# Ordering each engine's queue of a hybrid decoder block with a build-time list scheduler instead of hand-merged program order

## The chip, the cores and the metric

The kernel runs on the 8 cores of one Trainium2 chip. Each core works on two of the 16 sequences and the cores do not talk to each other. The metric is the device time of the slowest core, in microseconds (us). Executions of these kernels fall into two states: in the slow one the cores of a die show a lower granted TensorE clock and the time is longer (in the changed kernel 0.85 against 0.96, and 1918 against 1739 us). A median quoted is over all executions, slow ones included.

Names used below: PE is TensorE, DVE is VectorE, ACT is ScalarE, POOL is GpSimd, SP is SyncE, which here only issues DMAs. The traces here show each of them taking its queue in the order in which the program filled it. An operation at the head that waits for a semaphore holds up what stands behind it, ready or not: the example below is a wait of 41.55 us for one small constant.

## The reference

One layer, d_model 1024, 16 sequences of 2048 tokens behind 16 shared meta tokens:

```python
h = concat(meta_tokens, x)
u = rms_norm(h, norm_mix_g) @ w_in                     # 2576 columns
c_val, c_gate, q, k, v, g, gate_lr = split(u)
y_conv = conv_group(c_val, c_gate, ...)                # GLU, depthwise conv of 31, LayerNorm, swish
y_gla  = gla_group(q, k, v, g, gate_lr, ...)           # gated linear attention, 4 heads, state carried along
h = h + concat(y_conv, y_gla) @ w_out
h = h + (silu(n @ w_gate) * (n @ w_up)) @ w_down       # n = rms_norm(h, norm_ffn_g), hidden 2816
y = rms_norm(h, norm_final_g)
```

"Mixer" below is everything up to `w_out`, "feed-forward" the rest.

## The kernel before

A core handles 8 blocks of 512 tokens. Every operation is recorded with the buffers that it reads (R) and writes (W); the recorder derives its dependencies and appends it to its engine's queue at once, so a queue has the order of the Python program:

```python
    def add(self, eng, fn, R=(), W=(), dkey=None):
        op = Op(eng, fn, dkey is not None, dkey)
        ...                                    # deps: last writers and readers of R and W
        if eng == "pool" and fn is not None and dkey is None:
            if self.last_pool is not None:
                deps[id(self.last_pool)] = self.last_pool
            self.last_pool = op
        ...
        self.ops[eng].append(op)
```

The mixer of block b+1 does not depend on the feed-forward of block b, so the two are woven together by hand: lists of units with costs, merged so that the mixer's units fall between 15% and 93% of the feed-forward's cost.

```python
def merge(main, side, f0, f1):
    ...
    for c, fn in main:
        while i < len(side) and mt and done / mt >= f0 + (f1 - f0) * sdone / st_:
            out.append(side[i][1])
            ...
        out.append(fn)
        done += c
...
            plan = [fn for _, fn in mixer(0, blocks[0][0], True, True, False)]
            for b in range(nb):
                f = ffn(b % 2, blocks[b][0])
                m = mixer((b + 1) % 2, ...) if b + 1 < nb else []
                plan += merge(f, m, 0.15, 0.93) if m else [fn for _, fn in f]
            for fn in plan:
                fn()
```

A feed-forward unit, and the state chain of the mixer:

```python
P.add("pe", mm8(pg[:], ...), R=[Bwg] + Bx2T, W=[Bpg])            # 8 matmuls 128x512
P.add("pe", mm8(pu[:], ...), R=[Bwu] + Bx2T, W=[Bpu])
P.add("act", ... out=th, in_=pg, func=AF.Tanh)
P.add("dve", ... out=th, in0=th, in1=pg)                         # ftmp in the profile
P.add("dve", ... out=actT[:, j, :], in0=th, in1=pu)              # actT
# state chain, for each of four 128-token tiles
P.add("pool", ... out=Rbd[rows, t, :, hh, :], in0=S, in1=em2)    # twice
P.add("dve", ... out=U[:, hp, :], in0=S, in1=pkv)                # twice
P.add("dve", ... out=S[:, hp, :], in0=U)                         # twice
```

The program uses PSUM (the memory that matmuls write to) as eight tiles of 128x512 f32, called banks here: four for the feed-forward, four in rotation for the mixer. The feed-forward and the mixer each have a ring of four weight tiles in SBUF. The weights are read as f32 once, written back to HBM as bf16, and read as bf16 from then on. At the end of a block its four tiles of `h` are normalized and stored; then the `h` of the block after next is loaded into the same buffers.

Of the kernel before, what the change touches and what calls it, by code (L numbers as in the profile page):

```python
# [6 lines left out]
F32 = mybir.dt.float32  # L7
BF16 = mybir.dt.bfloat16
I32 = mybir.dt.int32
AF = mybir.ActivationFunctionType  # L10
# [14 lines left out]
LN_EPS = 1e-5  # L25
NWM, NWF = 4, 4
NW = NWM + NWF
RSQRT_MAGIC = 1597463007.0

W_GATE, W_VAL, W_Q, W_K, W_V, W_G, W_O, W_FG, W_FU, W_FD = 0, 2, 4, 5, 6, 8, 10, 14, 25, 36  # L30
# [3 lines left out]
class Buf:  # L34
    def __init__(self, name, psum=False):
        self.name = name
        self.lw = None
        self.rd = []
        self.psum = psum


class Op:
    __slots__ = ("eng", "fn", "deps", "sig", "ticket", "dma", "dkey", "dval")

    def __init__(self, eng, fn, dma, dkey):
        self.eng = eng
# [6 lines left out]
        self.dval = 0  # L53


class Prog:
    ENGS = ("pe", "act", "dve", "pool", "sp")

    def __init__(self):
        self.ops = {e: [] for e in self.ENGS}  # L60
        self.dcount = {}
        self.last_pool = None

    def add(self, eng, fn, R=(), W=(), dkey=None):
        op = Op(eng, fn, dkey is not None, dkey)
        deps = {}
        for b in R:
            if b.lw is not None:
                deps[id(b.lw)] = b.lw
            if b.psum:  # L70
                for r in b.rd:
                    if r.eng != eng:
                        deps[id(r)] = r
        for b in W:
            if b.lw is not None:
                deps[id(b.lw)] = b.lw
            for r in b.rd:
                deps[id(r)] = r
        if eng == "pool" and fn is not None and dkey is None:
            if self.last_pool is not None:  # L80
                deps[id(self.last_pool)] = self.last_pool
            self.last_pool = op
        deps.pop(id(op), None)
        op.deps = list(deps.values())
        for b in R:
            b.rd.append(op)
        for b in W:
            b.lw = op
            b.rd = []
        if op.dma:  # L90
            self.dcount[dkey] = self.dcount.get(dkey, 0) + 16
            op.dval = self.dcount[dkey]
        self.ops[eng].append(op)
        return op

    @staticmethod
    def _needs_wait(a, b):
# [43 lines left out]
def merge(main, side, f0, f1):  # L141

    mt = sum(c for c, _ in main)
    st_ = sum(c for c, _ in side)
    out, done, i = [], 0.0, 0
    sdone = 0.0
# [3 lines that stand above are left out]
            sdone += side[i][0]  # L150
            i += 1
        out.append(fn)
        done += c
    out.extend(fn for _, fn in side[i:])
    return out


def build_program(nseq, seqlen):
# [3 lines left out]
    nc = bass.Bass("TRN2", target_bir_lowering=False)  # L162
# [16 lines left out]
    out = nc.dram_tensor("out", [ntok, D], F32, kind="ExternalOutput").ap()  # L179
# [3 lines left out]
    with es:  # L183
        def sb(name, shape, dt=F32):
            return es.enter_context(nc.sbuf_tensor(name, list(shape), dt))
# [30 lines left out]
        sto = sb("sto", [128, 2, 6, 8])  # L216
        wring = [sb(f"wring{i}", [128, 2048], BF16) for i in range(NW)]
        gmix = sb("gmix", [128, D])
# [33 lines left out]
        def build(wseq):  # L252

            P = Prog()
# [33 lines left out]
            Bmt = [Buf(f"mt{i}") for i in range(4)]  # L288
            Bw = [Buf(f"w{i}") for i in range(NW)]
            Bwsc = [Buf(f"wsc{i}") for i in range(N_WT)]  # L290
# [110 lines left out]
            for s_ in range(4):  # L401
                P.add("dve", lambda e, s_=s_: e.tensor_copy(out=id4[s_ * 32:(s_ + 1) * 32, :],
                                                            in_=identf[s_ * 32:(s_ + 1) * 32, s_ * 32:(s_ + 1) * 32]),
# [24 lines left out]
            def newton_col(stt, Bst_, scale, eps):  # L428
# [3 lines left out]
                P.add("dve", lambda e: e.tensor_scalar(out=y.bitcast(I32), in0=a.bitcast(I32), scalar1=-0.5,  # L432
                                                       scalar2=RSQRT_MAGIC, op0=ALU.mult, op1=ALU.add), R=[Bst_], W=[Bst_])
                P.add("dve", lambda e: e.tensor_scalar(out=b, in0=a, scalar1=-0.5, scalar2=None, op0=ALU.mult),
# [8 lines left out]
            def newton_row(v, B_, scale, eps):  # L443
# [4 lines left out]
                P.add("dve", lambda e: e.tensor_scalar(out=y.bitcast(I32), in0=a.bitcast(I32), scalar1=-0.5,  # L448
                                                       scalar2=RSQRT_MAGIC, op0=ALU.mult, op1=ALU.add), R=[B_], W=[B_])
                P.add("dve", lambda e: e.tensor_scalar(out=b, in0=a, scalar1=-0.5, scalar2=None, op0=ALU.mult),  # L450
# [591 lines left out]
            plan = [fn for _, fn in mixer(0, blocks[0][0], True, True, False)]  # L1042
            for b in range(nb):
                f = ffn(b % 2, blocks[b][0])
                m = mixer((b + 1) % 2, blocks[b + 1][0], blocks[b + 1][1], False, True) if b + 1 < nb else []
                plan += merge(f, m, 0.15, 0.93) if m else [fn for _, fn in f]
            for fn in plan:
                fn()
            P.add("pool", None, W=Bh[0] + Bh[1] + Bwsc)
            return P, order  # L1050

        _, wseq = build(None)
        P, _ = build(wseq)
        P.finalize()
        esem = {e: es.enter_context(nc.semaphore(f"sem_{e}")) for e in Prog.ENGS}
        dsem = {k: es.enter_context(nc.semaphore(f"dsem_{k}")) for k in sorted(P.dcount)}
# [82 lines left out]
```

## Time and profile before

| before | us |
|---|---|
| median of the first 3 runs (the slowest is a slow one) | 2212.15 (2206.46 to 2273.65) |
| start to the first output store | 526.7 |
| block, store to store (middle of the run) | 254 to 256 |
| first store of the last block to the end | 17.6 |

From the page: the busy times, the busy share of PE in 40 slices with its granted clock, and the chain of waits that ended last. (Of 8498 matmuls 8340 have a record here.)

```profile
PE 1640.5 (74%) x8340; PEld 740.6 (34%) x8498; DVE 888.3 (40%) x1950; ACT 512.7 (23%) x808; POOL 201.7 (9%) x262
...
PE   0374768886897769877797768968697877977894
...
PEclk9885769998899889988898989989898988988997
...
PE 51%; DVE 19%; issue 13%; ACT 6%; DMA 5%; SPq 2%; POOL 2%; DVEq 1%; ACTq 0%; POOLq 0%
```

PE is the busiest engine and yet stands still a quarter of the time, in every slice a little, and its granted clock is below 0.9 in 22 of the 40 slices.

How PE loses time in a block, from its timeline:

```profile
1180.85 0.64 PE L836 MATMUL ps<-v_tm,k_tm 128*64 128x128 bf16 x16 [0.83 <-DVE k_tm L796]
1181.65 3.40 PE L486 MATMUL ps<-x2T,wring 128*128 128x512 bf16 x15 [0.16 <-issue]
1184.98 0.40 PE L808 MATMUL ps<-q_in,k_in 64*128 64x128 bf16 x8
1188.81 3.57 PE L486 MATMUL ps<-wring,xT 128*128 128x512 bf16 x8 [3.43 <-DVE U L851]
1198.59 1.86 PE L1011 MATMUL ps<-wring,actT 128*128 128x512 bf16 x4 [6.20 <-DVE actT L995]
```

The gate projection at 1188.81 waits 3.43 us for a bank that DVE's U operations free. After it, eight matmuls take 3.57 us at a granted clock of 0.50 (elsewhere eight take 1.89 us at 1.00), and then PE waits 6.20 us until DVE has made the last actT. DVE's timeline of the same stretch shows why actT is late:

```profile
1186.10 0.80 DVE L851 SCALAR_TENSOR_TENSOR U<-S,emid,ps 128x128 f32<-128x128 f32 x2
1187.08 0.68 DVE L855 TENSOR_SCALAR S<-U,csb 128x128 f32<-128x128 f32 x2 [0.18 <-DVE U L851]
...
1192.58 0.80 DVE L851 SCALAR_TENSOR_TENSOR U<-S,emid,ps 128x128 f32<-128x128 f32 x2
1194.15 2.79 DVE L855 TENSOR_SCALAR S<-U,csb 128x128 f32<-128x128 f32 x2 [0.77 <-POOL Rbd L845]
1196.86 0.67 DVE L993 SCALAR_TENSOR_TENSOR ftmp<-ftmp,ps 128x512 f32<-128x512 f32 x1
1197.64 0.69 DVE L995 SCALAR_TENSOR_TENSOR actT<-ftmp,ps 128x512 bf16<-128x512 f32 x1
```

The feed-forward's two operations, 1.4 us of work that PE needs, stand behind the whole state chain of the mixer, which itself pauses for POOL.

The start has its own loss. SP's queue, then the DVE operation that waited for it (start, length, what, and in brackets the idle time before it and what ended it):

```profile
22.55 30.82 SPq L326 DMA_DIRECT2D wsc<-wring  x8
...
55.66 0.43 SPq L353 DMA_DIRECT2D gng<-gla_norm_g  x1
```

```profile
58.27 0.17 DVE L410 TENSOR_SCALAR gb<-gb 128x2 f32<-128x2 f32 x1 [41.55 <-DMA gng<-gla_norm_g]
```

Eight write-backs, each waiting for its weight tile, stand ahead of five small constants. DVE waits 41.55 us for the last one, and the norms, and so PE (first matmul at 62.72 us), wait behind that DVE operation.

### The profile page before, as it was taken

The numbers are of one execution on the slowest core, as the hardware profiler recorded it, in microseconds if no ns is written. First come the engines' busy times: TensorE is split into PE (matmuls) and PEld (weight loads), VectorE is DVE, ScalarE is ACT, GpSimd is POOL, SyncE is SP. The second block draws the span as 40 slices with busy tenths as digits, with TensorE's granted clock in tenths as the row PEclk, the third lists the DMA queues.
The fourth block names the chain that finished last, engine by engine and source line by source line (L and its number), as shares of the span: only waits on it lengthen the run. The fifth ranks groups of instructions, "written<-read, shape, count | busy, mean of one in ns | idle before, by whom it ended". The sixth has DMA issues, their size and how long they took to land.

```text
span 2205.6 us, 27514 instructions; the slowest of 8 cores (2185.8 to 2205.6 us)
## 1 busy us (share of the span) xinstructions
PE 1640.5 (74%) x8340; PEld 740.6 (34%) x8498; DVE 888.3 (40%) x1950; ACT 512.7 (23%) x808; POOL 201.7 (9%) x262
## 2 busy tenths in 40 slices
PE   0374768886897769877797768968697877977894
PEld 0231323332333324333343333433243333433341
DVE  1225332544336342454325443363425443254422
ACT  0131222212231132312231122312222122312210
POOL 1012000300011000210002000110002000110000
PEclk9885769998899889988898989989898988988997
DMA  9242358775432245224342344323452343422442
GB/s 229 63 107 67 81 152 193 188 179 184 133 113 100 96 153 175 96 82 147 118 163 83 121 160 145 114 78 115 143 183 77 105 161 113 140 79 84 151 154 86
DMA packets 93488, 281.93 MB, mean 128 GB/s; under 512 B 12576, under 2 KB 29344, under 8 KB 93344
## 3 DMA queue, kind: packets, MB, share of 16 engines
q1 hardware_dynamic: 76928, 220.84, 30.6%
q0 software_dynamic: 16416, 59.32, 11.6%
q8 instruction: 72, 1.18, 0.2%
q14 instruction: 72, 0.59, 0.1%
HBM read 245.70 MB, written 41.94 MB: 130 GB/s over the span
## 4 chain that ended last, share of the span: by engine, by line
PE 51%; DVE 19%; issue 13%; ACT 6%; DMA 5%; SPq 2%; POOL 2%; DVEq 1%; ACTq 0%; POOLq 0%
PE ps L486 35%; PE ps L1011 10%; DMA wring<-wpack 4%; PE ps L631 2%; SPq L584 2%; DVE y_tm L905 2%; ACT xn_tm L462 1%; POOL Rbd L845 1%; PE ps L649 1%; DVE stn L437 1%; DVE xn_tm L465 1%; DVEq L131 1%; DVE S L855 1%; DVE csb L678 1%; PE ps L477 1%
## 5 line engine op out<-in xcount | busy, mean ns | idle before, releaser
L486 PE MATMUL ps<-x2T,wring 128*128 128x512 bf16 x2739 | 664.4, 399 | 93.2 <-DVE ftmp L993 69.3
L486 PEld LDWEIGHTS ps<-x2T,wring 128*128 128x128 bf16 x2816 | 282.6, 102 | 462.9 <-issue 182.9
L1011 PE MATMUL ps<-wring,actT 128*128 128x512 bf16 x1370 | 342.0, 405 | 55.1 <-DVE actT L995 43.3
L993 DVE SCALAR_TENSOR_TENSOR ftmp<-ftmp,ps 128x512 f32<-128x512 f32 x176 | 120.8, 686 | 401.6 <-ACT ftmp L992 401.6
L1011 PEld LDWEIGHTS ps<-wring,actT 128*128 128x128 bf16 x1408 | 142.9, 103 | 240.1 <-issue 103.3
L477 PE MATMUL ps<-ident,xn_tm 128*128 128x128 bf16 x520 | 50.0, 253 | 223.8 <-DVE stn L430 133.4
L992 ACT ACTIVATE ftmp<-ps 128x512 f32<-128x512 f32 x176 | 104.0, 595 | 426.2 <-PE ps L486 419.6
L486 PE MATMUL ps<-xT,wring 128*128 128x512 bf16 x751 | 194.0, 413 | 11.1 <-ACT xT L480 9.2
L486 PE MATMUL ps<-wring,xT 128*128 128x512 bf16 x497 | 134.5, 417 | 30.0 <-DVE U L851 29.1
L995 DVE SCALAR_TENSOR_TENSOR actT<-ftmp,ps 128x512 bf16<-128x512 f32 x176 | 121.1, 688 | 67.3 <-PE ps L486 63.3
L486 PE MATMUL ps<-wring,yT 128*128 128x512 bf16 x503 | 130.6, 411 | 0.7 <-issue 0.2
L477 PEld LDWEIGHTS ps<-ident,xn_tm 128*128 128x128 bf16 x520 | 39.5, 113 | 238.9 <-issue 234.1
L486 PEld LDWEIGHTS ps<-xT,wring 128*128 128x128 bf16 x768 | 80.0, 105 | 116.0 <-issue 43.1
L486 PEld LDWEIGHTS ps<-wring,xT 128*128 128x128 bf16 x512 | 52.6, 104 | 98.8 <-issue 48.7
L577 DVE SCALAR_TENSOR_TENSOR vT<-mtmp,ps 128x512 bf16<-128x512 f32 x32 | 22.0, 688 | 147.4 <-issue 86.9
L486 PEld LDWEIGHTS ps<-wring,yT 128*128 128x128 bf16 x512 | 52.9, 104 | 67.8 <-issue 21.3
L1035 POOL DMA_DIRECT2D out<-h_0 x8 | 4.7, 587 | 727.5 <-DVE h_0 L1032 727.5
L917 PE MATMUL ps<-ident,y_tm 128*128 128x128 bf16 x128 | 14.3, 244 | 72.0 <-DVE y_tm L905 72.0
L631 PE MATMUL ps<-rep,wcv 128*32 128x512 bf16 x1024 | 61.2, 388 | 4.0 <-DMA rep<-vT 4.0
L1019 DVE TENSOR_TENSOR h_0<-h_0,ps 128x512 f32<-128x512 f32 x16 | 11.0, 688 | 129.8 <-PE ps L1011 129.8
L769 POOL TENSOR_TENSOR rep<-rep,mtmp 128x512 f32<-128x512 f32 x32 | 44.6, 1393 | 200.5 <-PE ps L655 196.8
L774 ACT ACTIVATE mtmp<-rep 128x512 f32<-128x512 f32 x32 | 20.2, 630 | 171.5 <-DVE rep L771 171.5
(180 smaller groups left out, 1408.6 us busy)
## 6 DMA issues: line engine op xcount, KB each, us to landing
wring<-wsc SPq DMA_DIRECT2D x336, 512.0 KB, 4.1
wring<-wpack POOLq DMA_DIRECT2D x48, 512.0 KB, 8.4
wsc<-wring SPq DMA_DIRECT2D x48, 512.0 KB, 4.8
rep<-vT SPq DMA_DIRECT2D x256, 67.5 KB, 3.0
h_0<-xin POOLq DMA_DIRECT2D x8, 512.0 KB, 7.2
h_1<-xin POOLq DMA_DIRECT2D x8, 512.0 KB, 7.1
h_2<-xin POOLq DMA_DIRECT2D x8, 512.0 KB, 7.0
h_3<-xin POOLq DMA_DIRECT2D x8, 512.0 KB, 8.4
```

The lines of the kernel that those rows point to most:

```text
L131: eng.wait_ge(s, v)
L437: P.add("dve", lambda e: e.scalar_tensor_tensor(out=t_, in0=y, scalar=b, in1=y, op0=ALU.mult, op1=ALU.mult), R=[Bst_], W=[Bst_])
L477: ins = e.transpose(out=ptb[:, kc, :], in_=xn_tm[i][:, kc * 128:(kc + 1) * 128], identity=ident[:])
L486: ins = e.matmul(pt_ap, lhsT=lhs(kc), rhs=rhs(kc), start=(kc == 0), stop=(kc == KC - 1))
L584: P.add("sp", lambda e, s_=s_, g=g, c0=c - 1: e.dma_start(out=rep[s_ * 32:(s_ + 1) * 32, c0:c0 + 2, g, :], in_=vT[g * 32:(g + 1) * 32, c0: ...
L631: ins = e.matmul(pcv[g * 32:(g + 1) * 32, :], lhsT=wcv[:, c, g, a, :], rhs=rep[:, c, g, 4 * a:4 * a + T], start=(a == 0), stop=(a == 7))
L769: P.add("pool", lambda e: e.tensor_tensor(out=y, in0=y, in1=mu[:], op=ALU.subtract), R=[Bycv[c], Bmu], W=[Bycv[c]])
L905: P.add("dve", lambda e, hd=hd, hsl=hsl: e.scalar_tensor_tensor(out=y_tm[i][:, hsl], in0=po[:, hsl], scalar=y[:, hd:hd + 1], in1=sg[i][:, ...
L992: P.add("act", lambda e: e.activation(out=th[:], in_=pg[:], func=AF.Tanh, scale=0.5), R=[Bpg], W=[Bth])
L993: P.add("dve", lambda e: e.scalar_tensor_tensor(out=th[:], in0=th[:], scalar=1.0, in1=pg[:], op0=ALU.add, op1=ALU.mult), R=[Bpg, Bth], W=[ ...
L995: P.add("dve", lambda e: e.scalar_tensor_tensor(out=actT[:, j, :], in0=th[:], scalar=0.5, in1=pu[:], op0=ALU.mult, op1=ALU.mult), R=[Bpu, ...
L1011: ins = e.matmul(ps[t][:], lhsT=actT[:, j, t * 128:(t + 1) * 128], rhs=wd3[:, j - 4 * s_, :], start=(j == 0), stop=(j == NJ - 1))
```

## The change

The recorder now only collects operations. Running each operation's closure against a `Meter` gives it a rough duration from its shapes. Then a list scheduler simulates the five queues and the DMA: at each step it takes the engine that can act first and, of that engine's ready operations, the one with the lowest rank. The rank is the place in the same hand-merged plan. Dependencies and the rotation of buffers still come from program order, and only the order inside each queue is new. No operation, byte or buffer of the program is added or removed (the compiled kernel has 14 more loads of ACT's tables, see the last section).

```diff
+class Meter:
+    ...
+            if name == "dma_start":
+                self.nbytes += n * o.shape[0] * (2 if kw["in_"].dtype == BF16 else 4)
+                self.cost += 0.6 if len(o.shape) > 2 else 0.4
+            elif self.eng == "pe":
+                ...
+                self.cost += max(n, 64) / 2400.0 * (4 if fp else 1) * (rows / 128.0 if rows < 128 else 1.0)
+            elif self.eng == "act":
+                self.cost += 0.25 + n / 1400.0 + (0.19 if kw.get("accum_out") is not None else 0.0)
+    ...
-        self.ops[eng].append(op)
+        op.rank = (self.rank, len(self.all))
+        m = Meter(eng)
+        if fn is not None:
+            fn(m)
+        op.cost, op.nbytes = m.cost, m.nbytes
+        self.all.append(op)
         return op
+
+    def schedule(self):
+        ...
+        while n < len(self.all):
+            ...                                # e: the engine that can act first, at t
+            _, o = heapq.heappop(avail[e])     # its ready operation of lowest rank
+            free[e] = t + o.cost + 0.01
+            if o.dma:
+                dma_free = max(dma_free, free[e]) + o.nbytes / DMA_RATE      # DMA_RATE = 185e3
+                end = dma_free + 2.0
+            else:
+                end = free[e]
+            ...
+            self.ops[e].append(o)
+            ...                                # its users become ready at end + a small latency
 ...
-            for fn in plan:
+            for i, fn in enumerate(plan):
+                P.rank = float(i)
                 fn()
 ...
+        nc.model_us = P.schedule()
         P.finalize()
```

The chain that kept POOL's computing operations in order is now made from the scheduled order.

More of the change, by code (lines that the diff above doesn't have):

```diff
@@ L1 @@
 import contextlib
+import heapq
 import numpy as np
@@ L27 @@
 NW = NWM + NWF
+DMA_RATE = 185e3
 RSQRT_MAGIC = 1597463007.0
@@ L42 @@
 class Op:
-    __slots__ = ("eng", "fn", "deps", "sig", "ticket", "dma", "dkey", "dval")
+    __slots__ = ("eng", "fn", "deps", "sig", "ticket", "dma", "dkey", "dval", "rank", "cost", "lat", "nbytes", "users", "left",
+                 "ready")
     def __init__(self, eng, fn, dma, dkey):
@@ L53, in __init__, with __getattr__, f @@
         self.dval = 0
+class Meter:
+    def __init__(self, eng):
+        self.eng = eng
+        self.cost = 0.0
+        self.nbytes = 0
+    def __getattr__(self, name):
+        def f(*args, **kw):
+            o = kw["out"] if "out" in kw else args[0]
+            n = 1
+            for d in o.shape[1:]:
+                n *= d
+            if name == "dma_start":
+                self.nbytes += n * o.shape[0] * (2 if kw["in_"].dtype == BF16 else 4)
+                self.cost += 0.6 if len(o.shape) > 2 else 0.4
+            elif self.eng == "pe":
+                fp = name == "matmul" and kw["lhsT"].dtype == F32
+                rows = o.shape[0] if name == "matmul" else 128
+                self.cost += max(n, 64) / 2400.0 * (4 if fp else 1) * (rows / 128.0 if rows < 128 else 1.0)
+            elif self.eng == "act":
+                self.cost += 0.25 + n / 1400.0 + (0.19 if kw.get("accum_out") is not None else 0.0)
+                if kw.get("func") == AF.Ln:
+                    self.cost += 1.0
+            elif self.eng == "dve":
+                if name == "tensor_tensor_scan":
+                    self.cost += 0.1 + n * 3.1e-3
+                else:
+                    if name == "tensor_reduce":
+                        n = 512
+                    self.cost += 0.16 + n / 960.0 * (0.5 if o.dtype == BF16 and name == "tensor_copy" else 1.0)
+            else:
+                self.cost += 0.15 + n * (2.5e-3 if o.dtype == F32 or name == "tensor_tensor" else 1.3e-3)
+            return None
+        return f
 class Prog:
@@ L61, in __init__ @@
         self.dcount = {}
-        self.last_pool = None
+        self.all = []
+        self.rank = 0.0
     def add(self, eng, fn, R=(), W=(), dkey=None):
@@ L78, in add @@
                 deps[id(r)] = r
-        if eng == "pool" and fn is not None and dkey is None:
-            if self.last_pool is not None:
-                deps[id(self.last_pool)] = self.last_pool
-            self.last_pool = op
         deps.pop(id(op), None)
@@ L92, in add @@
             op.dval = self.dcount[dkey]
-        self.ops[eng].append(op)
-        return op
+        op.rank = (self.rank, len(self.all))
[4 more added lines that the diff above has]
+        self.all.append(op)
+        return op
+    def schedule(self):
+        for o in self.all:
+            o.users, o.left, o.ready = [], len(o.deps), 0.0
+        for o in self.all:
+            for d in o.deps:
+                d.users.append(o)
+        pend = {e: [] for e in self.ENGS}
+        avail = {e: [] for e in self.ENGS}
+        free = {e: 0.0 for e in self.ENGS}
+        dma_free = 0.0
+        last_pool = None
+        for o in self.all:
+            if not o.left:
+                heapq.heappush(pend[o.eng], (0.0, o.rank, o))
+        n = 0
+        while n < len(self.all):
+            best = None
+            for e in self.ENGS:
+                if avail[e]:
+                    t = free[e]
+                elif pend[e]:
+                    t = max(free[e], pend[e][0][0])
+                else:
+                    continue
+                if best is None or t < best[0]:
+                    best = (t, e)
+            t, e = best
+            while pend[e] and pend[e][0][0] <= t + 1e-9:
+                r, k, o = heapq.heappop(pend[e])
+                heapq.heappush(avail[e], (k, o))
+            _, o = heapq.heappop(avail[e])
[3 more added lines that the diff above has]
+                end = dma_free + 2.0
+            else:
+                end = free[e]
+            if e == "pool" and o.fn is not None and not o.dma:
+                if last_pool is not None and last_pool not in o.deps:
+                    o.deps.append(last_pool)
+                last_pool = o
+            self.ops[e].append(o)
+            n += 1
+            for u in o.users:
+                lat = 0.05 if u.eng == e and not o.dma else (0.25 if e == "pe" else 0.12)
+                u.ready = max(u.ready, end + lat)
+                u.left -= 1
+                if not u.left:
+                    heapq.heappush(pend[u.eng], (u.ready, u.rank, u))
+        return max(free.values())
     @staticmethod
@@ L1046, in build @@
                 plan += merge(f, m, 0.15, 0.93) if m else [fn for _, fn in f]
-            for fn in plan:
+            for i, fn in enumerate(plan):
+                P.rank = float(i)
                 fn()
+            P.rank = 1e9
             P.add("pool", None, W=Bh[0] + Bh[1] + Bwsc)
```

## The prediction

> **What bounds it now.** TensorE order, not TensorE work. The page gives PE 74% busy, DVE 40%, ACT 23%, POOL 9%, granted clock 0.88. By stage (busy time by window, PE's timeline):
> - 0 to 251 us: first mixer alone. PE starts at 62.7 us: VectorE waits 41.5 us for the last constant (gng), whose DMA sits behind eight weight write-backs on the SP queue (22.6 to 53.4 us). Later PE stands still about 70 us in pieces (16 us at the rep DMAs, 2 to 8 us each in the state, output and norm chains).
> - 251 to 553 us: first feed-forward + second mixer, 302 us, DMA share 0.69; its weights are read as f32 and written back.
> - 553 to 2034 us: six blocks of 247 us, PE busy 197 of them, clock 0.90. From 850 to 1096 us I add some 50 us of PE idle: waits for U, k_tm, actT, y_tm, xn_tm, ftmp, up to 6 us each, an in-order PE head while the other stream's matmuls were ready.
> - 2034 to 2205 us: tail, PE nearly dense.
> About 750 128x512 matmuls per block at 0.216 us (dense stretch) are 162 us, the rest about 24: an estimate of 186 us of PE work per block.
>
> **The change.** No operation, byte or buffer is added or removed; PSUM and tile rotation stay fixed by program order. Only the order inside each queue changes (the order comparison): constants ahead of the write-backs on SP; about 25 feed-forward groups on PE, with the transposes spread between them, before the next mixer's projections; down projections fill up to the last transposes; VectorE interleaves Newton chains. The scheduler's costs agree with the trace (128x512: DVE 0.69 us, ACT 0.60, POOL 1.4), but it takes full TensorE clock, so the queues will drift and some stalls stay.
>
> **Clock.** [...] after the idle start weight loads are 0.43 us apart, later 0.216. So filled gaps also raise the clock. [...] 2100 to 2150 us, dense, shows 1.00 on this core[...].
>
> **Sum (estimates).**
> - Start: 251 to about 165 us (43 from the constants, about 40 of the 70 us of stalls).
> - First feed-forward: 302 to about 255 us; share x time = 208 us of DMA is its floor.
> - Six blocks: 247 to about 211 us each (60% of 60 us of idle and cold clock): 1266 us.
> - Tail: 171 to about 165 us.
> With launch, about 6 us: about 1860; for drift and somewhat lower clock I put **1880 us** (15% faster), range **1785 to 2000**. Faster by over 2%: 0.95; within 2%: 0.03; slower: 0.02.
>
> **What would show it.** First PE instruction near 15 to 20 us; busy time of DVE, ACT, POOL unchanged within 2%; PE busy share 85 to 92%, granted clock 0.94 or more; output stores 205 to 220 us apart in the middle (247 now); waits of the transposes L477 (224 us now) below 60; DMA share in the first feed-forward near 0.85; bytes equal.
>
> **What would make it wrong.** [...] drift, an engine's head waiting for late PE work while ready work lies behind it; the output store, reload and norm chain (about 35 us) not covered; the first stage bound by weight DMA.

The marked cuts are rules on the TensorE clock that came from no trace of this case, and a risk that rested on them. 165 + 255 + 1266 + 165 + 6 = 1857 us ("about 1860"), 1880 with the cushion. The weight loads 0.43 and 0.216 us apart stand in the trace of before at 79 to 81 and from 82 us; the granted clock of the middle block was 0.89 before and 0.99 after.

## More of the kernel before

The busy time by window, for the first mixer, the first feed-forward with the second mixer, one whole block, and the last feed-forward (columns: length, then busy us and instructions of each engine, granted clock, DMA share, GB/s):

```profile
core 0: us, PE busy (x) PEld busy (x) DVE busy (x) ACT busy (x) POOL busy (x), PEclk, DMA share, GB/s
0.00:251.00 251.00, 102.07 (x626) 50.70 (x634) 84.52 (x212) 52.56 (x85) 35.13 (x51) 0.82 0.45 111
251.00:526.70 275.70, 214.57 (x1060) 95.63 (x1080) 103.67 (x237) 64.78 (x102) 33.38 (x52) 0.87 0.69 168
1040.10:1294.30 254.20, 201.91 (x1028) 90.62 (x1048) 109.36 (x240) 63.15 (x99) 21.86 (x28) 0.89 0.38 126
2061.00:2205.60 144.60, 108.38 (x486) 48.74 (x496) 44.37 (x68) 16.54 (x28) 4.29 (x8) 0.89 0.39 133
```

In the whole block, PE idles for 254.2 - 201.9 = 52.3 us, and no other engine is half busy. The block is cut from the first output store of one block to that of the next, in POOL's timeline (start, length, what, and in brackets the idle time before it and what ended it):

```profile
1040.13 0.60 POOL L1035 DMA_DIRECT2D out<-h_0  x1 [96.40 <-DVE h_0 L1032]
...
1294.26 0.60 POOL L1035 DMA_DIRECT2D out<-h_0  x1 [94.58 <-DVE h_0 L1032]
```

## The result

The changed kernel's first four runs were 1738.95, 1737.81, 1740.41 and, in the slow state, 1918.42 us: a median of 1739.7. A ratio is the mean time of one kernel's fast runs over that of the other's fast runs of the same rounds, so it is not quite the ratio of the medians quoted; here it is 0.787 (95% interval 0.784 to 0.790). The result is correct against the reference. The predicted 1880 us, and its range down to 1785, were too slow.

The page after, the lines that answer to those above:

```profile
PE 1538.3 (89%) x8498; PEld 711.8 (41%) x8498; DVE 845.8 (49%) x1950; ACT 526.2 (30%) x822; POOL 192.9 (11%) x262
...
PE   1676997878899989999899989999899989999993
...
PEclk9897999999999999999999999999999999999997
...
PE 73%; DVE 8%; DMA 7%; issue 6%; ACT 2%; SPq 2%; DVEq 1%; POOL 0%; ACTq 0%; POOLq 0%
```

By window, the same four stages:

```profile
core 1: us, PE busy (x) PEld busy (x) DVE busy (x) ACT busy (x) POOL busy (x), PEclk, DMA share, GB/s
0.00:173.90 173.90, 95.51 (x635) 48.38 (x636) 80.42 (x220) 54.45 (x88) 33.06 (x55) 0.88 0.72 172
173.90:413.20 239.30, 206.09 (x1096) 93.22 (x1096) 100.45 (x233) 65.11 (x102) 32.52 (x47) 0.96 0.79 185
816.60:1012.40 195.80, 187.51 (x1050) 86.81 (x1049) 103.93 (x240) 65.07 (x101) 20.55 (x25) 0.99 0.53 162
1599.00:1737.40 138.40, 105.21 (x478) 46.75 (x476) 41.46 (x64) 15.94 (x27) 4.32 (x8) 0.90 0.41 137
```

In the whole block PE idles for 195.8 - 187.5 = 8.3 us. The block lost 58.4 us: 44.0 us of idle time, and 14.4 us of busy time, in which the same matmuls now run at a granted clock of 0.99 instead of 0.89 (scaling the busy time by the two clocks alone would give 20 us). In POOL's timeline the stores that bound it:

```profile
816.62 0.60 POOL L1130 DMA_DIRECT2D out<-h_0  x1 [67.50 <-DVE h_0 L1127]
...
1012.42 0.60 POOL L1130 DMA_DIRECT2D out<-h_0  x1 [69.96 <-DVE h_0 L1127]
```

PE and DVE in the stretch that answers to the one shown before (scores, state, first down projection):

```profile
932.50 0.64 PE L931 MATMUL ps<-v_tm,k_tm 128*64 128x128 bf16 x16
933.07 1.90 PE L581 MATMUL ps<-x2T,wring 128*128 128x512 bf16 x8
934.90 0.40 PE L903 MATMUL ps<-q_in,k_in 64*128 64x128 bf16 x8
936.02 3.61 PE L1106 MATMUL ps<-wring,actT 128*128 128x512 bf16 x16 [0.72 <-DVE S L950]
939.47 1.89 PE L581 MATMUL ps<-wring,xT 128*128 128x512 bf16 x8
```

```profile
737.81 0.35 DVE L946 SCALAR_TENSOR_TENSOR U<-S,emid,ps 128x128 f32<-128x128 f32 x1 [0.44 <-PE ps L931]
738.08 0.68 DVE L1088 SCALAR_TENSOR_TENSOR ftmp<-ftmp,ps 128x512 f32<-128x512 f32 x1
738.67 0.34 DVE L946 SCALAR_TENSOR_TENSOR U<-S,emid,ps 128x128 f32<-128x128 f32 x1
739.12 0.29 DVE L950 TENSOR_SCALAR S<-U,csb 128x128 f32<-128x128 f32 x1
739.63 0.69 DVE L1090 SCALAR_TENSOR_TENSOR actT<-ftmp,ps 128x512 bf16<-128x512 f32 x1 [0.22 <-PE ps L581]
```

DVE (here one block earlier) puts the feed-forward's two operations between those of the state chain. PE runs a down projection first and the gate projection after it, when its bank is free: the 3.43 and 6.20 us have become 0.72.

At the start SP now issues the last constant at 5.64 us, and the write-backs come after:

```profile
5.64 1.07 SPq L448 DMA_DIRECT2D gng<-gla_norm_g  x1
25.80 3.75 SPq L421 DMA_DIRECT2D wsc<-wring  x2
```

Where the 468 us between the two profiled executions (2205.6 and 1737.4 us) came from, with boundaries at the output stores:

| stage | before | after | saved |
|---|---|---|---|
| to the first output store | 526.7 | 413.2 | 113.5 |
| the next six block intervals together | 1534.3 | 1185.8 | 348.5 |
| last interval and end | 144.6 | 138.4 | 6.2 |

Of the prediction's other signs: bytes are equal (281.9 MB), the first matmul is at 20.1 us (15 to 20 had been given), PE's busy share is 89% and the granted clock 0.96, as foretold. The stores are 195 to 196 us apart in the middle, where 205 to 220 had been given. PE's idle time before the transposes fell from 224 to 81 us, not below 60. The DMA share in the first feed-forward is 0.79, not 0.85. And DVE's busy time fell by 4.8%, POOL's by 4.4% and ACT's rose by 2.6%, where all three were to stay within 2% (see the last section).

### The profile page after: what moved, and what is told of

It is laid out like the page before. It is cut to its first block, busy times and chain, and to the rows that moved or that the text cites. A ratio compares the mean times of both kernels' runs of the same rounds, so it can differ in the third digit from the quotient of the medians.

```text
span 1737.4 us, 27522 instructions; the slowest of 8 cores (1726.5 to 1737.4 us)
## 1 busy us (share of the span) xinstructions
PE 1538.3 (89%) x8498; PEld 711.8 (41%) x8498; DVE 845.8 (49%) x1950; ACT 526.2 (30%) x822; POOL 192.9 (11%) x262
## 4 chain that ended last, share of the span: by engine, by line
PE 73%; DVE 8%; DMA 7%; issue 6%; ACT 2%; SPq 2%; DVEq 1%; POOL 0%; ACTq 0%; POOLq 0%
PE ps L581 49%; PE ps L1106 14%; PE ps L726 3%; DMA h_0<-xin 2%; DMA wring<-wpack 2%; PE ps L572 2%; SPq L679 2%; PE ps L744 2%; DVE xn_tm L560 1%; DMA wsc<-wring 1%; PE ps L639 1%; DVE y_tm L1000 1%; DVE stn L532 1%; DMA h_3<-pre 1%; DVE stn L534 1%
## 5 line engine op out<-in xcount | busy, mean ns | idle before, releaser
L581 PE MATMUL ps<-x2T,wring 128*128 128x512 bf16 x2816 | 646.7, 387 | 19.8 <-DVE ftmp L1088 9.1
L581 PEld LDWEIGHTS ps<-x2T,wring 128*128 128x128 bf16 x2816 | 274.8, 100 | 365.2 <-issue 62.0
L1106 PE MATMUL ps<-wring,actT 128*128 128x512 bf16 x1408 | 319.8, 382 | 20.5 <-DMA wring<-wpack 9.7
L1106 PEld LDWEIGHTS ps<-wring,actT 128*128 128x128 bf16 x1408 | 135.9, 98 | 182.2 <-issue 30.6
L581 PE MATMUL ps<-xT,wring 128*128 128x512 bf16 x768 | 171.7, 380 | 2.6 <-DVE vT L668 1.1
L581 PE MATMUL ps<-wring,xT 128*128 128x512 bf16 x512 | 120.2, 386 | 2.8 <-ACT actT L712 1.4
L581 PE MATMUL ps<-wring,yT 128*128 128x512 bf16 x512 | 118.6, 382 | 2.7 <-ACT yT L1015 2.7
L940 POOL TENSOR_TENSOR Rbd<-S,emid 64x256 bf16<-64x256 f32 x64 | 43.0, 671 | 473.7 <-ACT emid L781 345.1
L575 ACT ACTIVATE x2T<-ps 128x1024 bf16<-128x1024 bf16 x32 | 32.4, 1023 | 83.2 <-PE ps L572 80.4
L970 ACT ACTIVATE sg<-ps 128x512 f32<-128x512 f32 x32 | 19.1, 597 | 126.5 <-PE ps L581 90.8
```

Of the source, the lines that this page charges most:

```text
L575: P.add("act", lambda e: e.activation(out=dst, in_=ptb, func=AF.Copy), R=[Bpt], W=[Bdst])
L581: ins = e.matmul(pt_ap, lhsT=lhs(kc), rhs=rhs(kc), start=(kc == 0), stop=(kc == KC - 1))
L940: P.add("pool", lambda e, t=t, hh=hh, rows=rows: e.tensor_tensor(out=Rbd[rows, t, :, hh, :], in0=S[rows, :, :], in1=em2[rows, :, t].unsque ...
L1106: ins = e.matmul(ps[t][:], lhsT=actT[:, j, t * 128:(t + 1) * 128], rhs=wd3[:, j - 4 * s_, :], start=(j == 0), stop=(j == NJ - 1))
```

## The experiments

All ran on the eight cores and gave correct results. Each profile is of a fast run. "Block" is the mean of the second to sixth interval between the output stores of successive blocks in that profile, "first store" the time of the first of them. The variants of the scheduler change the order of queues and nothing else; one of them (e16) also a dependency.

| run | queues free to reorder | median us | ratio to before | first store | block |
|---|---|---|---|---|---|
| before | none | 2205 to 2243 | 1 | 526.7 | 255.3 |
| e1 | none; constants first | 2174.3 | 0.986 | 499.6 | 255.8 |
| e4 | POOL, SP | 2143.8 | 0.970 | 469.3 | 256.0 |
| e9 | DVE | 2100.6 | 0.952 | 479.5 | 247.2 |
| e2 | PE | 1977.2 | none given | 499.7 | 218.9 |
| e10 | PE, DVE | 1874.9 | 0.851 | 449.8 | 214.3 |
| e3 | all but PE | 1946.7 | 0.882 | 420.8 | 232.0 |
| e5 | all but DVE | 1931.5 | 0.875 | 463.3 | 219.2 |
| e17 | all but ACT | 1904.2 | 0.839 | 436.2 | 212.5 |
| e13 | all but POOL, SP | 1847.6 | 0.838 | 441.9 | 211.0 |
| e18 | all but POOL | 1786.5 | 0.810 | 435.1 | 201.4 |
| after | all | 1739.7 | 0.787 | 413.2 | 195.6 |
| e6 | all, random costs | 1746.1 | 0.790 | 412.0 | 199.6 |
| e14 | all, PE costs doubled | 1814.9 | 0.823 | 393.3 | 212.9 |
| e15 | all, PE costs halved | 1852.5 | 0.840 | 440.2 | 214.7 |
| e7 | all, uniform costs | 1924.6 | 0.872 | 446.7 | 223.8 |
| e12 | all, mixer 10 ranks earlier | 1770.0 | 0.802 | 412.0 | 201.0 |
| e8 | all, mixer 40 ranks earlier | 1807.0 | 0.819 | 413.6 | 207.4 |
| e11 | all, DMA rate 350 | 1686.4 | 0.764 | 380.2 | 194.3 |
| e16 | as e11, finer history dependency | 1674.7 | 0.759 | 374.4 | 193.0 |

(The medians of e17 and e2 lie between two fast runs and two slow ones: 1847.5 and 1851.4 us fast in e17, 1961.1 and 1962.8 in e2. For e2 its fast runs over those of before are about 0.889. The profiled run of e18 was 17 us slower than its other four; its first interval, which is not in the average, is 221.9 us. One interval of e15 is 224.8 us; its other four average 212.2.)

Two questions were put. Which queue's order makes the blocks short: PE's (theory A, the prediction's) or those of the engines that empty PSUM (rival B)? And why was so little lost to drift between plan and chip, for which the prediction had taken away 40% of the recoverable time?

### e1: the constants ahead of the write-backs, by hand

```diff
+            cload(wg2[:], wg2_d)
+            ...                                # gb, convw4, cvec, gng
             if wseq is not None:
                 for r in range(2):
                     for n in range(RING[r][1]):
                         wissue(r, n)
-            cload(wg2[:], wg2_d)
-            ...
```

> The kernel before with one change by hand: the five small constant loads are queued ahead of the eight weight write-backs on SP; all else in program order. If the constants are worth what the prediction says (about 43 us, all on the critical path of the start): about 43 us less than before, first PE instruction near 20 us, and the six block periods stay at 256 us. Rival: the start is bound by the DMA of the first weights, then the first PE instruction is as early but the first output store moves by less than 20 us.

The ratio of 0.986 (0.983 to 0.989: clear of noise, though less than 2%) is about 32 us, the first store came 27 us earlier, the blocks did not move, and the first matmul ran at 25.4 us instead of 62.7. So PE started 37 us earlier and gave about 10 of them back: it waited 21.4 us, not 16.4, for the copies of the conv input, and then 5.4 us for the second half of them. Of the 43 us expected, 27 to 32 came; the cause was right, and the rest went into a wait that stood behind the first one.

### e2, e3, e4: PE alone, all but PE, DMA queues alone

The scheduler gets a set of queues that must keep program order. An operation of such a queue becomes ready only when its predecessor in the queue has been placed, so the result is consistent.

```diff
+HELD = ('act', 'dve', 'pool', 'sp')
 ...
+        nxt, prev = {}, {}
+        for o in self.all:
+            if o.eng in HELD:
+                if o.eng in prev:
+                    nxt[id(prev[o.eng])] = o
+                    o.left += 1
+                prev[o.eng] = o
 ...
+            u = nxt.get(id(o))
+            if u is not None:
+                u.ready = max(u.ready, free[e])
+                u.left -= 1
+                if not u.left:
+                    heapq.heappush(pend[u.eng], (u.ready, u.rank, u))
```

e3 has `HELD = ('pe',)`, e4 `('pe', 'act', 'dve')`.

> The list scheduler with ACT, DVE, POOL and SP held to program order; only PE is free. Theory A (the prediction's: an in-order PE head blocks ready matmuls) expects at least two thirds of the gain, under 1900 us, with block periods of about 215 us. Rival B (the queues that empty PSUM, above all VectorE, must be reordered too, since a PE that runs ahead meets banks that an in-order VectorE has not emptied) expects over 2050 us and periods over 240 us.

> The reverse: PE held to program order, the other four queues free. Theory A expects little beyond the start: 2100 to 2170 us, block periods 245 us or more. Rival B expects most of the gain, under 1900 us. If both this and the run with PE alone keep over half of the blocks lost, PE and the other queues gain only together.

> Only POOL and SP free, that is the DMA queues and the POOL chain; PE, ACT and DVE in program order. Expected by both theories: the start's gain alone, about 2150 us, block periods within 5 us of 256. If it is under 2100 us, the order of DMA issue matters in the steady blocks and both theories miss it.

Neither theory held. PE alone takes 36 us from the block (255.3 to 218.9) and the four others without PE take 23 (to 232.0); all five take 60. In the blocks the two parts nearly add up. The start belongs to the other queues: with PE held the first store is at 420.8 us, near the 413.2 of the full change, while PE alone reaches 499.7. The DMA queues alone change no block (e4's mean of 256.0 contains one interval of 264.4; the other four are 253 to 254) but bring the first store to 469.3 us, 30 us better than the constants alone.

### e5, e9, e10, e13, e17, e18: which of the other queues

e5 holds only DVE. e9 frees only DVE, e10 PE and DVE; e13 holds POOL and SP, e17 ACT, e18 POOL.

> All queues free but VectorE, which is held to program order. PE alone gave block periods of 218.5 us, all but PE 232, all 195.6 (before 255.7). If VectorE's order is what the other queues give (theory: the interleaved Newton and state chains), periods of 214 us or more, near the run with PE alone, and about 1900 us. Rival: ACT's order or the DMA queues give it, then under 202 us and about 1780 us.

> Only VectorE free; PE, ACT, POOL and SP in program order. If VectorE is the one queue behind the 24 us a block that the queues other than PE gave together: periods of 230 to 234 us and about 2060 us. If VectorE's order helps only when ACT's moves with it: over 245 us a block.

> PE and VectorE free, ACT, POOL and SP in program order. If PE and VectorE are the whole of the steady blocks: periods of 195 to 200 us, with the start still slow (first output store near 490 us, since the constants stay behind the write-backs), about 1820 us. If ACT or the DMA queues matter beside them: periods over 205 us.

> PE, ACT and VectorE free, POOL and SP in program order. If ACT is the missing partner of VectorE (each empties PSUM for the other: tanh, then the product), periods of 195 to 199 us, with the start slower than in the changed kernel, about 1790 us. If the DMA queues and POOL are the partner: periods near 214 us.

> All free but ACT. If every queue is a link of the same chain: 10 to 25 us a block more than 195.6, so 206 to 221 us. If ACT, busy only a third of the block, has slack: under 200 us.

> All free but POOL. If the 15.5 us a block of POOL and SP together are POOL's (its state and layer-norm operations in program order delay the state chain): 208 to 212 us a block. If they are SP's (order of weight loads and replication copies): under 199 us.

With DVE held, the block is 219.2 us, the 218.9 of PE alone: without DVE's order, those of ACT, POOL and SP add nothing to PE's. That looked as if DVE were the whole of the second part, and it is not. DVE alone gives 8 us (247.2), which is the other branch of e9's expectation and not the 21 to 25 of the first, and PE with DVE reaches 214.3 and not 195 to 200. Freeing ACT beside them (e13) brings 3 us more (211.0), so ACT is not the one missing partner either. Holding one queue out of five costs: PE 36 us a block, DVE 24, ACT 17, POOL and SP 15, of which POOL alone 6 (between the two expectations of e18). The other 10 would be SP's by difference; SP was not held alone.

PE's waits in one block of each run (`--waits`, us) show which wait each order removes:

| waits of PE for DVE's | before | e2 (PE free) | e5 (DVE held) | e3 (PE held) | e9 (DVE free) | after |
|---|---|---|---|---|---|---|
| ftmp, actT and U (feed-forward, state chain) | 19.7 | 15.0 | 12.4 | 1.0 | 4.9 | 0.8 |
| stn and xn_tm (norms) | 18.3 | 3.0 | 8.6 | 23.8 | 25.8 | 5.0 |

The waits behind the state chain stay while DVE keeps program order, and a free PE does not hide them; the waits for the norms stay while PE keeps program order, since only PE can put other matmuls there. With ACT held (e17) one wait of 9.3 us for a norm and one of 3.1 us for ftmp are back.

So every one of these orders counts. An operation that the mixer or the feed-forward needs passes several engines in turn, and one in-order queue on the way puts part of the old wait back. DVE alone shows the other side: it removes most of its own waits, but those for the norms grow (18.3 to 25.8), which is why freeing it gives 8 us and holding it costs 24.

### e6, e7, e14, e15: wrong durations in the plan

```diff
-        op.cost, op.nbytes = m.cost, m.nbytes
+        op.cost, op.nbytes = m.cost * 2.0 ** (((len(self.all) * 7919) % 1001) / 500.0 - 1.0), m.nbytes    # e6
+        op.cost, op.nbytes = (0.5 if fn is not None else 0.0), m.nbytes                                  # e7
+        op.cost, op.nbytes = m.cost * (2.0 if eng == "pe" else 1.0), m.nbytes                            # e14; 0.5 in e15
```

> All queues free, but every cost in the scheduler multiplied by a fixed pseudo-random factor between one half and two. The prediction took away 40% of the gain for drift between plan and chip. If the order needs right durations, this loses much: block periods over 215 us, over 1880 us. If the order only needs to be a sensible one, because queues have slack at most heads, periods stay under 203 us and the time under 1800 us.

> All queues free, but every operation costs 0.5 us in the scheduler, so it knows only the dependencies: a group of eight matmuls (1.7 us) counts like a 0.15 us column operation. If durations matter: over 215 us a block. If dependencies and rank are enough: under 203 us. I expect this to be worse than the noise, about 210 us a block, since the ratio between engines is wrong in one direction.

> All queues free, PE costs doubled in the scheduler, as if the clock were always halved. If a one-sided clock error makes the order bad (the prediction's drift): periods over 205 us, over 1800 us. If slack absorbs it: within 2% of 1739 us.

> All queues free, PE costs halved in the scheduler, so that it believes the other engines to be the bottleneck. Drift theory: over 1800 us. Slack theory: within 2%. Since uniform costs, which make PE too cheap by 3.4 against a small VectorE operation too dear by 3, lost 185 us, I expect this direction to be the worse one, 1780 to 1850 us.

Random errors of up to a factor of two cost 6 us in 1740 (ratio 0.790 against 0.787, whose intervals overlap) and 4 us a block. One-sided errors of the same size cost 17 us a block in the one direction and 19 in the other (17 without e15's one long interval), 75 and 113 us in all. Uniform costs, which distort the ratio between engines further, cost 28 us a block (223.8 us, where about 210 was expected). The order therefore does not need exact durations, but it needs the balance between the engines. So each expectation was right for one kind of error: e6 met the bounds set for slack in the plan, e14 those set for drift, and e15's time came out 2.5 us above its stated range of 1780 to 1850.

### e8, e12: other priorities

```diff
-                P.rank = float(i)
+                P.rank = i + (BIAS if getattr(fn, "side", False) else 0.0)      # side: set by merge on mixer units; BIAS -40 in e8, -10 in e12
```

> All queues free, but mixer operations get priority over feed-forward ones (rank 40 units earlier) in place of the hand-merged ranks. If the merge by hand no longer matters once there is a scheduler, the same time within 1% (1722 to 1757 us). If the mixer run first leaves nothing to fill with at the end of a block, periods rise to over 200 us. A gain would show as periods under 192 us.

> All queues free, mixer ranks moved ahead by 10 units, a quarter of the run that lost 67 us. If the hand-merged ranks are near an optimum, between 1739 and 1770 us, periods 195 to 200 us. If a little more mixer priority helps, under 1730 us.

Mixer priority loses 30 us at 10 ranks (e12: block 201.0, just outside its 195 to 200) and 67 us at 40 (e8: 207.4). The hand merge was not made superfluous: it is the scheduler's priority, and it was near a good one. The other direction, feed-forward first, was not run.

### e11, e16: a better plan for the start

The build prints what the scheduler simulates: first store at 538.5 us, blocks of 198.4, end at 1872.9. The blocks agree with the chip's 195.6, the start is far off the chip's 413.2. Its DMA is a single pipe of 185 bytes per ns. The plan built on that let the second mixer run ahead in the first feed-forward and left all 176 matmuls of its down projections to the end, in one piece (the 48 of the expectation are only the first group of them). e11 sets `DMA_RATE = 350e3`.

> All queues free, the scheduler's DMA rate raised from 185 to 350 bytes per ns. The scheduler plans the first output store at 538 us with 185, the chip has it at 413, so its plan for the first feed-forward is wrong: it lets the second mixer run ahead and leaves 48 down projections that wait for weights. A right rate should keep feed-forward and mixer interleaved there: 10 to 20 us less than the changed kernel (1720 to 1730 us), block periods the same. Rival: the first feed-forward is bound by DMA whatever the order, then within 5 us of 1739.

It gained more than expected: 1686.4 us, ratio 0.764 (0.762 to 0.767) against 0.787, with the first store 33 us earlier, the first block interval 14 us shorter (193.8 instead of 207.9 us) and 1.3 us a block after that. By window, the changed kernel at 300 to 400 us, and then e11:

```profile
300.00:350.00 50.00, 43.17 (x226) 20.47 (x225) 29.35 (x82) 14.19 (x23) 3.69 (x7) 0.93 0.77 183
350.00:400.00 50.00, 37.65 (x162) 15.53 (x160) 2.48 (x4) 0.58 (x1) 4.23 (x8) 0.97 1.00 217
```

```profile
300.00:350.00 50.00, 48.38 (x266) 23.50 (x273) 32.10 (x103) 9.69 (x17) 8.57 (x15) 1.00 0.96 223
350.00:400.00 50.00, 45.79 (x232) 21.35 (x234) 26.58 (x58) 15.65 (x25) 4.78 (x9) 1.00 0.84 243
```

From 350 to 400 us the changed kernel has the DMA full (1.00), PE busy for only 37.65 us of 50, waiting for weights in 7.4 of the other 12.35 us, and DVE and ACT almost without work. In e11 the mixer's work lies between the down projections and PE is busy 45.79 us.

In e11 PE still waits at the start. e16 keeps the record of the 32 history columns per pair of channel groups, so that the meta tokens' writes for groups 2 and 3 do not wait for the copies of groups 0 and 1:

```diff
-            Bhist = Buf("hist")
+            Bhist = [Buf(f"hist{i}") for i in range(2)]
-                                    op1=ALU.mult), R=[Bpv, Bth], W=[Bhist])
+                                    op1=ALU.mult), R=[Bpv, Bth], W=[Bhist[c // 2]])
-                                        R=[BvT[c - 1], BvT[c], Bhist] + ...
+                                        R=[BvT[c - 1], BvT[c], Bhist[c // 2]] + ...
 # all other uses name both
```

> The 350 rate plus one dependency made finer: the record of the 32 history columns is kept for each pair of channel groups, so that the meta tokens' writes for groups 2 and 3 no longer wait for the copies of groups 0 and 1. In the trace of the 350 run PE waits 23.7 us at 53 to 77 us for exactly that write. If that wait is the cause: about 20 us less, 1660 to 1672 us. If the copies themselves bind that stretch: within 5 us of 1686.

PE's timeline at that place, of e11 and of e16:

```profile
76.71 1.01 PE L581 MATMUL ps<-actT,wring 128*128 128x128 bf16 x8 [23.73 <-DVE vT L668]
```

```profile
72.38 3.19 PE L581 MATMUL ps<-wring,actT 128*128 128x512 bf16 x7 [15.43 <-DMA wring<-wpack]
```

The wait for the history is gone and a wait for the f32 weights has taken most of its place: the stretch was bound twice. The median is 1674.7 us, 12 us under e11 where 14 to 26 were expected, and the first store is 5.8 us earlier. The ratios to before, 0.759 (0.758 to 0.761) and 0.764 (0.762 to 0.767), come from two jobs; e16 is the fastest version measured, and its lead over e11 is small beside what may differ between jobs. Both beat the changed kernel by about 3%.

## Why the prediction was wrong, point by point

- **What bounds the kernel: right.** "TensorE order, not TensorE work" is what the windows show: the block lost 44.0 of its 52.3 us of PE idle time, and PE's share rose from 74 to 89%.
- **The step that failed is "Six blocks: 247 to about 211 us each (60% of 60 us of idle and cold clock)".** Measured: 255.7 to 197.6 us on average over the six, 58 us saved each and not 36, which makes 348.5 and not 216 us. Two terms of it were mis-sized. First, 247 us was not a block: it was a sixth of a window with arbitrary ends, and the stores of the same profile, in which the block can be read off, are 254 to 258 us apart. Against the prediction's own 186 us of PE work there were 70 us to gain, not 60. Second, the 60%: 60 of those 70 us came back in the middle blocks (255.3 to 195.6): 86%.
- **Why the discount for drift was wrong.** The prediction gave as its reason that the plan "takes full TensorE clock, so the queues will drift". e14 and e15 show what a one-sided clock error of two does cost, 17 to 19 us a block: less than the 24 us that the discount took off, for an error far larger than a clock of 0.89 would have been. And even the smaller error was not there: the block ran at a granted clock of 0.99. Over the runs whose block was windowed, its clock is higher where its PE idle time is shorter: 50 us idle and 0.90 in e9, 34 and 0.93 in e3, 19 to 30 and 0.94 to 0.98 in the eight runs with blocks of 211 to 224 us, 8 to 12 and 0.97 to 1.00 where blocks are under 203. So with the gaps filled the clock came near to what the plan had assumed. That the plan's block of 198.4 us comes so close to the chip's 195.6 is partly luck: its DMA rate was too low. Built again with e11's rate (no chip is needed), the plan prints blocks of 185.2 us, and the chip took 194.3. About 9 us a block are thus left for drift and whatever else the plan does not know. The prediction named that link between gaps and clock in its paragraph on the clock and did not carry it into the sum, where the clock was still counted as drift. Errors that are not one-sided cost 4 us a block (e6).
- **Theory A, an in-order PE head, was somewhat over half of the mechanism.** The prediction described the waits as "an in-order PE head while the other stream's matmuls were ready". Its paragraph on the change lists new orders on VectorE and SP too, but ties no part of the blocks' gain to them. PE's order alone gives 36 of the 60 us (e2). The rest needs DVE, ACT and the DMA queues too (e3, e5, e17, e13), as DVE's timeline of before shows, with the feed-forward's operations behind the state chain.
- **The start was overestimated.** 86 + 47 = 133 us were predicted to the end of the first feed-forward and 113.5 were saved to the first store. The first mixer's share was near (first feed-forward matmuls at 173.9 us, predicted 165). "43 from the constants" was 32 when done alone (e1). In the first feed-forward the plan's own wrong DMA rate left 33 us on the table (e11), so a floor set by the DMA was too simple: with the DMA busy for 0.79 of the stage it was the order again.
- **The cushion.** The terms summed to about 1857 us; about 23 us were added "for drift and somewhat lower clock". The clock rose to 0.96 over the whole span. Of the 140 us between 1880 and 1740, 132 are what the blocks saved beyond the forecast, less 20 that the start fell short, plus 23 of cushion and 4 of launch.
- **The main risk did not come about in fast runs.** It was a lower clock through the dense blocks. The changed kernel's middle block ran at 0.99; the one slow run in four, with 0.85 on one die, is taken up in the last section.

Not settled: what in SP's order is worth about 10 us a block (only by difference, e13 and e18), and how much of the last 8 us of idle in a block could be ordered away.

## What to carry to other kernels

When two independent streams share in-order queues, order all queues together from one simulated plan: here PE's order alone was worth 36 us a block, all five queues 60, and one queue left in program order cost between 6 and 36. Get the balance between engines and the DMA rate right and do not worry about the rest: random factors of two cost about 0.4%, a TensorE clock wrong by two 4 to 6.5%, and correcting one DMA constant gained 3%. Before predicting such a change, read the length of a block between two marks of the profile that recur, and do not discount for a slow clock that the change itself removes (here 0.89 became 0.99 in the block).

## What else the traces show

- The clock. A group of eight matmuls takes 3.57 us after a 3.43 us gap, at a granted clock of 0.50, and 1.89 us in a dense stretch, at 1.00. The block's mean clock rose from 0.89 to 0.99 when its gaps were filled.
- The slow state. In the profiled run of the changed kernel all eight cores ran the same block with PE 95 to 96% busy at a granted clock of 0.99, and the means over the whole span were 0.96 to 0.97 in each of its three fast runs. One run in four was slow, with a mean clock of 0.85 on one die (the other: 0.96) and 1918 us, 10% over the fast ones. Slow runs of the kernel before took 2237 to 2363 us, 1 to 7% more. What brings the slow state about is not shown, and whether a denser kernel loses more to it is open: slow runs of the variants cost 2 to 13%.
- What stood ahead. The gaps of PE lead to its waits for DVE, and there they stop: what made the releasing operation late was DVE's queue order, and holding that order costs 24 of the 60 us a block (e5). The step that was needed is to look at what stood ahead of the releasing operation in its own queue (1.4 us of feed-forward work behind 10 us of state chain, 1186 to 1197 us).
- DVE's busy time. A pair of state updates took 2.79 us before, beside two POOL operations of 1.26 us, where other pairs of that stretch take 0.68 us. Over the kernel the mean of this operation fell from 517 to 288 ns and that of the cumulative sum from 1627 to 1224 ns, together 21 of the 42 us by which the new order changed DVE's busy time of 888 us. Why these operations took longer was not tested.
- ACT's tables. A load takes 1283 ns in the traces. The scheduler has no cost for one, and there are 17 loads before and 31 after. The 14 more make 18 us of loading on an engine that is a third busy; whether any of them is on the critical path was not tested.
